# Moving one modulation vector's load and sums from a feed-forward to the token mixer of the second layer

## The chip, the cores and the metric

The kernel runs on one core of one Trainium2 chip. The metric is the device time of one execution in microseconds (us), as the median of several runs. Five engines work side by side, each through its own instructions in order: TensorE (PE, matmuls, with weight loads shown apart as PEld), VectorE (DVE), ScalarE (ACT), GpSimd (POOL) and SyncE (SP), which here only issues DMA transfers from HBM.

## What is computed

Two layers of a decoder trunk on 256 rows of width 1024, in f32. In each layer three sub-layers follow each other: a SwiGLU feed-forward, a token mixer with two attention branches, and a second feed-forward. Each is wrapped in a modulated norm and a gated residual:

```python
c_act = jax.nn.silu(c)
for l in range(DEPTH):
    mod = c_act @ w_ada[l] + b_ada[l]                 # 9 vectors of 1024
    sh1, sc1, g1, sh2, sc2, g2, sh3, sc3, g3 = jnp.split(mod, N_MOD, axis=-1)
    x = x + 0.5 * g1[:, None, :] * swiglu(modulate(x, sh1, sc1), ffn1_gate[l], ffn1_up[l], ffn1_down[l])
    x = x + g2[:, None, :] * token_mix(modulate(x, sh2, sc2), ...)
    x = x + 0.5 * g3[:, None, :] * swiglu(modulate(x, sh3, sc3), ffn2_gate[l], ffn2_up[l], ffn2_down[l])
return rms_norm(x) * final_norm
```

`modulate(x, shift, scale)` is `rms_norm(x) * (1 + scale) + shift`. The nine vectors of `mod` are numbered 0 to 8 in the code. The change is about number 6 of the second layer, `sh3`, which is first needed by the norm ahead of that layer's second feed-forward.

## The kernel before

**Products.** Every f32 matrix is used as a high and a low part. A weight is loaded into a buffer named `raw` (128 x 2048 values at most, usually 1 MB, 4 buffers in a ring), and `split_unit` makes the two parts of it: ScalarE copies the high one (`whi`, line 177), VectorE subtracts for the low one (`wlo`, line 179). PE then does three products per pair of tiles (line 105). A `raw` buffer is free for the next load when its splits are done.

**Modulation vectors.** `ada_half` makes half a vector (512 values). It loads two blocks of 1 MB of `w_ada` (line 216) into the same ring of `raw` buffers, and VectorE adds 4 columns of each to an accumulator `acc`, so 8 sums per half (line 222 for the first, which only multiplies and is shorter, line 224 for the others). `finish` then adds over the partitions: for the gate vectors (2, 5, 8) by two products with ones, for the others by a column sum, 8 tiny matmuls on PE `tr<-acc,ones`, and three small VectorE instructions (`mcol`, `cs`, `col`). A vector so takes 4 loads, 16 sums and, if it isn't a gate, 2 column sums.

**Where they run.** Each sub-layer is given a list of halves (`HALVES`), and `ada_load` makes a generator of it. The sub-layer's code calls `ada_step` at fixed places, mostly just after it has issued the load of a weight, and each call runs the generator to its next `yield`. In a feed-forward the steps stand in the gate and up products (13 of them in the second layer's first feed-forward) and then one behind the load of each block of the down weight (`stream_units`, line 435, `ada_every` = 1); one step issues a load and then its sums. What is left runs before the norm (`ada_flush`). The feed-forward named has 10 halves before the change, so 20 loads, of which the last 7 are issued in the down projection. In the token mixer the flag `ada_lag` is set: `ada_half` yields between the load and its sums, and once more behind the sums. Its first four steps stand behind the loads of the 408-column products (two: gates and latent query, buffers `cqs`) and of the 288-column products (two: latent key and value, `cks`); the next ones stand at lines 718, 752 and 802, two in the query products, and so on. Before the change the first layer's token mixer has 2 halves there (vector 7), and the second layer's none.

**The order on the engines.** Instructions of each engine are put in order by a scheduler ahead of time, from the program's order and its own estimate of durations; on the chip each engine keeps that order and waits on semaphores. SP's queue of loads is in order too: a load that waits for a free `raw` buffer holds up those behind it.

Of the kernel before, what the change touches and what calls it, by code (L numbers as in the profile page):

```python
# [77 lines left out]
def hybrid_trunk(ctx, tc, t, out):  # L78
# [20 lines left out]
    def trps():  # L99
        return psum.tile([P, 512], F32, name="tr", tag="tr", bufs=2)  # L100
# [3 lines left out]
    def mm(o, a, b, start, stop):  # L104
        last_mm[0] = nc.tensor.matmul(o, a, b, start=start, stop=stop)  # L105
# [29 lines left out]
    def raw_tile():  # L135
        return raws.tile([P, 2048], F32, name="raw", tag="raw")
# [49 lines left out]
    def column_sums(ps, vec, a, start, stop):  # L186

        av = a.rearrange("p (j i r) -> p j i r", j=4, i=4)
        for i in range(4):
            mm(ps[32 * i:32 * i + 32, :P].rearrange("p (j r) -> p j r", j=4), vec, av[:, :, i, :], start, stop)  # L190

    def pick_columns(ps):
        m = small.tile([P, 4, 32], F32, name="mcol", tag="mcol", bufs=1)
        nc.vector.tensor_tensor(m, ps[:, :P].rearrange("p (j r) -> p j r", j=4),
                                colmask[:, None, :].to_broadcast([P, 4, 32]), ALU.mult)
        cs = small.tile([P, 4], F32, name="cs", tag="cs", bufs=2)
        nc.vector.tensor_reduce(cs, m, AX.X, ALU.add)
        return cs

    def add_bias(l, ch, n, cs):  # L200
        if (l, ch) not in mods:
            mods[l, ch] = small.tile([P, KD], F32, name="col", tag="col", bufs=8)
        nc.vector.scalar_tensor_tensor(mods[l, ch][:, n * 4:n * 4 + 4], cs, 1.0 if ch in (1, 4, 7) else 0.0,
                                       bcols[:, l, ch * 8 + n * 4:ch * 8 + n * 4 + 4], ALU.add, ALU.add)

    def ada_half(l, ch, n):
        acc = keep.tile([P, 512], F32, name="acc", tag="acc", bufs=2)
        row = ch in (2, 5, 8)
        n0 = ch * D + n * 512
        wv = t["w_ada"][l].rearrange("(p j) n -> p j n", p=P)  # L210
        if row:
            nc.scalar.dma_start(binit[0:1, :], t["b_ada"][l:l + 1, n0:n0 + 512])
        for j in range(0, KD, 4):
            r = raw_tile()
            rv = r.rearrange("p (j n) -> p j n", j=4)
            nc.sync.dma_start(rv, wv[:, j:j + 4, n0:n0 + 512])
            if ada_lag[0]:
                yield
            for jj in range(4):
                cj = cact[:, j + jj:j + jj + 1]  # L220
                if j + jj == 0 and not row:
                    nc.vector.tensor_scalar_mul(acc, rv[:, jj, :], cj)
                else:
                    nc.vector.scalar_tensor_tensor(acc, rv[:, jj, :], cj, binit if j + jj == 0 else acc,  # L224
                                                   ALU.mult, ALU.add)
            yield
        if row:
            if n == 0:
                mods[l, ch] = keep.tile([P, D], F32, name="g", tag="g", bufs=2)
            hi, lo = (scr.tile([P, 512], F32R, name="acc%d" % i, tag="uf", bufs=2) for i in range(2))  # L230
            nc.scalar.activation(hi, acc, AF.Copy)
            nc.vector.tensor_tensor(lo, acc, hi.bitcast(F32), ALU.subtract)

            def finish():
                ps = trps()
                mm(ps, ones, hi, True, False)
                mm(ps, ones, lo, False, True)
                nc.scalar.activation(mods[l, ch][:, n * 512:(n + 1) * 512], ps, AF.Copy, scale=1.0 if ch == 5 else 0.5)
        else:
            def finish():  # L240
                ps = trps()
                column_sums(ps, ones[:, :32].bitcast(F32), acc, True, True)
                cs = pick_columns(ps)
                add_bias(l, ch, n, cs)
        ada_late.append(finish)

    ada_late = []
    ada_lag = [False]
    ada_gen = [None]

    def ada_load(chunks):
        def g():
            for l, ch, n in chunks:
                for _ in ada_half(l, ch, n):
                    yield
                    while ada_late:
                        ada_late.pop(0)()
            while ada_late:
                ada_late.pop(0)()
        ada_gen[0] = g()  # L260
# [858 lines left out]
    HALVES = lambda l, *chs: [(l, ch, n) for ch in chs for n in range(2)]  # L1119
# [15 lines left out]
    def start_norm(l, sub):  # L1135
        u = new_u()

        def post(hf):
            pending.append([DELAY[hf] + (sub == 1 and hf == 1), norm_mod(hf, u[0], u[1], mods[l, 3 * sub + 1], mods[l, 3 * sub],
                                                sub == 1 and hf == 1)])  # L1140
        return u, post
# [41 lines left out]
    for i, (l, sub) in enumerate(subs):  # L1183
        u = nxt
        if i + 1 < len(subs):
            state = {}

            def post(hf, state=state, ls=subs[i + 1]):
                if hf == 0:
                    state["u"], state["post"] = start_norm(*ls)  # L1190
                state["post"](hf)
        else:
            post = final_norm
        if sub == 0:
            ffn(l, 1, u[0], u[1], HALVES(l, 2, 3, 4, 5, 6), post,
                xn if l == 0 else None, small_columns if l == 0 else None)
        elif sub == 1:
            token_mix(l, u[0], u[1], HALVES(l, 7) if l == 0 else [], post)
        else:
            ffn(l, 2, u[0], u[1], HALVES(l, 8) + (HALVES(l + 1, 1, 0, 7) if l + 1 < DEPTH else []), post)  # L1200
        if i + 1 < len(subs):
            nxt = state["u"]
# [22 lines left out]
```

## Time and profile before

| what | value |
|---|---|
| median of 3 runs | 1177.66 us (1175.4 to 1183.46) |
| the profiled execution | 1180.38 us, its span from first to last instruction 1178.6 us |
| busy: PE, PEld, DVE, ACT | 97%, 86%, 80%, 54% of the span |
| bytes moved | 274.95 MB, 233 GB/s on average |
| mean granted TensorE clock | 0.995 of full speed |

The stages can be told by what PE multiplies. In the second layer the first feed-forward's down projection begins near 731 us and ends near 791, the token mixer's first products begin near 796, its 408-column products at 821, its 288-column products at 830, and the second feed-forward's down projection runs from 1111 to the end. The first layer's token mixer has its 408-column products at 247 and its 288-column products at 256, and the second feed-forward of that layer its down projection from 540 to 598. The times in the rows below are us from the start of the span. A recorded matmul is longer than the time to the next one's start, since they are pipelined; what a matmul costs in a row of them is the difference of two starts.

### The profile page before, as it was taken

To read this page: it belongs to the slowest core of one execution; us is meant where nothing else is said; L and a number is where in the kernel's file an instruction comes from. 1 tells how busy PE (TensorE), PEld (TensorE's weight loads), DVE (VectorE), ACT (ScalarE), POOL (GpSimd) and SP (SyncE) were. 2 spreads that over 40 slices of the span, in tenths; PEclk is the share of its full clock that TensorE was granted. 3 is DMA by queue.
4 is the path that set the end of the run, shared out by engine and by line. 5 is a ranking of instruction groups with operands and counts; after the bars stand their busy time and mean duration, and the time that the engine had idled before them with its cause. 6 is when DMAs were issued, how large, how long until landed. Compare 5 with 4: busy or idle time off the path is not lost.

```text
span 1178.6 us, 20227 instructions
## 1 busy us (share of the span) xinstructions
PE 1145.7 (97%) x7902; PEld 1007.8 (86%) x7902; DVE 938.5 (80%) x1889; ACT 641.2 (54%) x1156; POOL 2.6 (0%) x16
## 2 busy tenths in 40 slices
PE   4999999999999999999999999999999999999997
PEld 3799987789977889998879999877997778999985
DVE  4888899779897898799578879975888888865553
ACT  4444436647677564444455534356677756564441
POOL 0000000000000000000000000000000000000000
PEclk9999999999999999999999999999999999999999
DMA  9989999686823578989838979976574354986530
GB/s 327 325 295 306 318 357 330 218 223 182 249 73 108 181 230 303 315 272 323 293 119 286 314 250 347 336 253 170 148 215 108 108 170 152 305 252 212 184 138 36
DMA packets 201970, 274.95 MB, mean 233 GB/s; under 512 B 13613, under 2 KB 119815, under 8 KB 201875
## 3 DMA queue, kind: packets, MB, share of 16 engines
q1 hardware_dynamic: 201119, 273.02, 70.8%
q8 instruction: 62, 1.02, 0.3%
q10 hardware_dynamic: 756, 0.64, 0.2%
q14 instruction: 33, 0.27, 0.1%
HBM read 272.60 MB, written 1.05 MB: 232 GB/s over the span
## 4 chain that ended last, share of the span: by engine, by line
PE 60%; DVE 18%; DMA 14%; ACT 4%; issue 3%; SPq 1%; DVEq 0%; ACTq 0%
PE mm L105 52%; DVE wlo L179 8%; DVE acc L224 4%; DMA raw<-in_ffn_up 4%; DMA raw<-in_w_ada 4%; DMA raw<-in_ffn_down 3%; PE tr L108 3%; ACT whi L177 2%; PE sc L105 2%; PE po L105 2%; DMA raw<-in_ffn_gate 2%; PE tr L105 1%; DVE hf L497 1%; DVE hl L499 0%; DVE rtmp L455 0%
## 5 line engine op out<-in xcount | busy, mean ns | idle before, releaser
L179 DVE TENSOR_TENSOR wlo<-raw,whi 128x1024 fp32r<-128x1024 f32 (+5 forms) x400 | 423.4, 1074 | 125.0 <-ACT whi L177 122.2
L177 ACT ACTIVATE whi<-raw 128x1024 fp32r<-128x1024 f32 (+5 forms) x400 | 364.4, 936 | 231.2 <-PE mm L105 90.4
L105 PE MATMUL mm<-uhi,whi 128*128 128x256 f32 x1248 | 346.6, 278 | 0.0
L105 PE MATMUL mm<-uhi,wlo 128*128 128x256 f32 x1248 | 345.2, 277 | 0.7 <-DVE wlo L179 0.7
L105 PE MATMUL mm<-ulo,whi 128*128 128x256 f32 x1248 | 344.9, 276 | 0.0
L105 PEld LDWEIGHTS mm<-uhi,whi 128*128 128x128 f32 x1248 | 234.3, 188 | 2.7 <-issue 1.4
L105 PEld LDWEIGHTS mm<-uhi,wlo 128*128 128x128 f32 x1248 | 234.3, 188 | 1.1 <-DVE wlo L179 1.0
L105 PEld LDWEIGHTS mm<-ulo,whi 128*128 128x128 f32 x1248 | 234.5, 188 | 0.5
L224 DVE SCALAR_TENSOR_TENSOR acc<-raw,cact,acc 128x512 f32<-128x512 f32 x224 | 167.3, 748 | 6.6 <-DMA raw<-in_w_ada 3.7
L105 PE MATMUL mm<-wlo,hh 128*128 128x512 f32 x352 | 137.6, 391 | 2.1 <-DVE wlo L179 2.1
L105 PE MATMUL mm<-whi,hh 128*128 128x512 f32 x352 | 138.3, 393 | 0.0
L105 PE MATMUL mm<-whi,hl 128*128 128x512 f32 x352 | 137.1, 389 | 0.0
L105 PE MATMUL mm<-whi,uhi 128*128 128x512 f32 (+3 forms) x336 | 127.2, 380 | 3.4 <-ACT uhi L557 2.6
L105 PE MATMUL mm<-whi,ulo 128*128 128x512 f32 (+3 forms) x336 | 126.5, 377 | 1.3 <-DVE ulo L345 1.3
L105 PE MATMUL mm<-wlo,uhi 128*128 128x512 f32 (+3 forms) x336 | 125.7, 374 | 0.0
L498 ACT ACTIVATE hh<-hf 128x256 fp32r<-128x256 f32 x70 | 29.2, 417 | 103.7 <-DVE hf L497 103.7
L105 PEld LDWEIGHTS mm<-wlo,hh 128*128 128x128 f32 x352 | 66.1, 188 | 16.9 <-DVE wlo L179 3.6
L105 PEld LDWEIGHTS mm<-whi,hh 128*128 128x128 f32 x352 | 66.1, 188 | 15.2 <-ACT whi L177 0.9
L105 PEld LDWEIGHTS mm<-whi,hl 128*128 128x128 f32 x352 | 66.1, 188 | 13.6
L105 PEld LDWEIGHTS mm<-whi,uhi 128*128 128x128 f32 x336 | 63.7, 190 | 14.7 <-ACT uhi L557 3.0
L105 PEld LDWEIGHTS mm<-whi,ulo 128*128 128x128 f32 x336 | 64.0, 190 | 12.2 <-DVE ulo L345 3.2
L105 PEld LDWEIGHTS mm<-wlo,uhi 128*128 128x128 f32 x336 | 64.0, 190 | 9.3 <-issue 0.3
(248 smaller groups left out, 1328.9 us busy)
## 6 DMA issues: line engine op xcount, KB each, us to landing
raw<-in_w_ada SPq DMA_DIRECT2D x72, 1024.0 KB, 9.2
raw<-in_ffn_gate SPq DMA_DIRECT2D x41, 1024.0 KB, 6.1
raw<-in_ffn_up SPq DMA_DIRECT2D x41, 1024.0 KB, 6.0
raw<-in_ffn_down SPq DMA_DIRECT2D x40, 1024.0 KB, 8.2
raw<-in_w_in SPq DMA_DIRECT2D x18, 1024.0 KB, 5.5
raw<-in_w_in SPq DMA_DIRECT2D x16, 512.0 KB, 5.2
raw<-in_w_out SPq DMA_DIRECT2D x8, 1024.0 KB, 5.6
raw<-in_ffn_down SPq DMA_DIRECT2D x8, 512.0 KB
```

The lines of the kernel that those rows point to most:

```text
L105: last_mm[0] = nc.tensor.matmul(o, a, b, start=start, stop=stop)
L108: nc.tensor.transpose(o, a, ident)
L177: nc.scalar.activation(a, s, AF.Copy)
L179: nc.vector.tensor_tensor(b, s, a.bitcast(F32), ALU.subtract)
L224: nc.vector.scalar_tensor_tensor(acc, rv[:, jj, :], cj, binit if j + jj == 0 else acc, ALU.mult, ALU.add)
L497: nc.vector.tensor_tensor(hf32, ps[:, 256:], sg, ALU.mult)
L498: nc.scalar.activation(h[0][:, f, :], hf32, AF.Copy)
```

## The change

Vector 6 of the second layer leaves the list of that layer's first feed-forward (8 halves stay, 16 loads) and becomes the list of its token mixer, which had none. And in the token mixers the second of the two `yield`s goes: a step now does the sums of the load before and at once issues the next load, and one more `yield` at the end of the list takes the last column sum a step further on. So the four loads of a vector are issued in the first four steps there, where they took steps 1, 3, 5 and 7. This holds for the first layer's vector 7 and for the second layer's vector 6. In the feed-forwards the flag is off, and their steps are as before.

```diff
@@ ada_half
                     nc.vector.scalar_tensor_tensor(acc, rv[:, jj, :], cj, binit if j + jj == 0 else acc,
                                                    ALU.mult, ALU.add)
-            yield
+            if not ada_lag[0]:
+                yield
@@ ada_load
                     yield
                     while ada_late:
                         ada_late.pop(0)()
+            if ada_lag[0]:
+                yield
             while ada_late:
                 ada_late.pop(0)()
@@ the list of sub-layers
         if sub == 0:
-            ffn(l, 1, u[0], u[1], HALVES(l, 2, 3, 4, 5, 6), post,
+            ffn(l, 1, u[0], u[1], HALVES(l, *((2, 3, 4, 5, 6) if l == 0 else (2, 3, 4, 5))), post,
                 xn if l == 0 else None, small_columns if l == 0 else None)
         elif sub == 1:
-            token_mix(l, u[0], u[1], HALVES(l, 7) if l == 0 else [], post)
+            token_mix(l, u[0], u[1], HALVES(l, 7 if l == 0 else 6), post)
```

On SP, in the second layer's token mixer, the loads stood so before the change (the loads of the 408- and 288-column weights, small ones of the compression, and those of the next products):

```order
L435 DMA raw<-in_w_in 128x4x408
L776 DMA w_9340<-in_cmpk_w 64x64
L776 DMA w_9340<-in_cmpv_w 64x64
L435 DMA raw<-in_w_in 128x4x408
L435 DMA raw<-in_w_in 128x4x288 x2
L717 DMA raw<-in_w_in 128x8x256
L750 DMA raw<-in_w_in 128x8x128
L751 DMA raw<-in_w_in 128x8x128
```

and stand so in the changed kernel (lines behind the edits are 3 higher):

```order
L438 DMA raw<-in_w_in 128x4x408
L779 DMA w_9340<-in_cmpk_w 64x64
L779 DMA w_9340<-in_cmpv_w 64x64
L216 DMA raw<-in_w_ada 128x4x512
L438 DMA raw<-in_w_in 128x4x408
L216 DMA raw<-in_w_ada 128x4x512
L438 DMA raw<-in_w_in 128x4x288
L216 DMA raw<-in_w_ada 128x4x512
L438 DMA raw<-in_w_in 128x4x288
L216 DMA raw<-in_w_ada 128x4x512
L720 DMA raw<-in_w_in 128x8x256
```

One modulation load now stands behind each of the four weights. In the first layer's token mixer the same four places hold one each after the change, where before they held one behind the first and one behind the third weight, and two further on.

On VectorE, at the same place of the second layer, the low parts of the 408-column weights (128x816) and of the 288-column weights (128x576) and the copies out of PSUM (`gate`, `cqs`) stood in this order before:

```order
L179 TENSOR_TENSOR wlo<-raw,whi 128x816 x4
L179 TENSOR_TENSOR wlo<-raw,whi 128x576 x3
L694 TENSOR_SCALAR gate<-gate 128x24
L695 COPY cqs<-mm 128x384
L694 TENSOR_SCALAR gate<-gate 128x24
L695 COPY cqs<-mm 128x384
```

and in the changed kernel in this one, from the second 128x816 split on:

```order
L224 SCALAR_TENSOR_TENSOR acc<-raw,cact,acc 128x512
L179 TENSOR_TENSOR wlo<-raw,whi 128x816
L224 SCALAR_TENSOR_TENSOR acc<-raw,cact,acc 128x512
L179 TENSOR_TENSOR wlo<-raw,whi 128x816
L224 SCALAR_TENSOR_TENSOR acc<-raw,cact,acc 128x512 x2
L222 TENSOR_SCALAR acc<-raw,cact 128x512
L224 SCALAR_TENSOR_TENSOR acc<-raw,cact,acc 128x512 x3
L179 TENSOR_TENSOR wlo<-raw,whi 128x576
L224 SCALAR_TENSOR_TENSOR acc<-raw,cact,acc 128x512 x2
L179 TENSOR_TENSOR wlo<-raw,whi 128x576
L224 SCALAR_TENSOR_TENSOR acc<-raw,cact,acc 128x512 x2
```

The sums of the second load stand between the 408-column splits, all four of the third ahead of the first 288-column split, and those of the fourth around the second one; a third 288-column split and the copies follow. The first layer's token mixer has the same order there.

## Rows read from the trace of the kernel before

**Rows 1.** Busy time of the engines, from the page: us, share, instructions.

```profile
PE 1145.7 (97%) x7902; PEld 1007.8 (86%) x7902; DVE 938.5 (80%) x1889; ACT 641.2 (54%) x1156; POOL 2.6 (0%) x16
```

**Rows 2.** Table by windows: stretch, length, busy us (instructions) by engine, clock, DMA share, GB/s.

```profile
731.00:796.00 65.00, 64.18 (x301) 51.39 (x296) 55.43 (x84) 31.65 (x46) 0.00 (x0) 1.00 0.86 297
540.00:603.00 63.00, 62.42 (x297) 50.52 (x296) 42.49 (x63) 30.70 (x43) 0.00 (x0) 1.00 0.67 235
247.30:263.50 16.20, 15.48 (x97) 15.22 (x96) 9.46 (x17) 7.86 (x15) 0.00 (x0) 1.00 0.83 219
821.30:836.60 15.30, 15.30 (x98) 15.26 (x97) 7.23 (x12) 7.80 (x15) 0.00 (x0) 1.00 0.72 168
1110.70:1170.00 59.30, 59.30 (x264) 49.11 (x263) 26.46 (x33) 21.39 (x28) 0.00 (x0) 1.00 0.31 107
```

**Rows 3.** PE by time, second layer's first feed-forward: start, us, what, [idle before <-releaser].

```profile
768.35 0.39 PE L105 MATMUL mm<-whi,hl 128*128 128x512 f32 x1
...
769.10 0.50 PE L105 MATMUL mm<-whi,hh 128*128 128x512 f32 x1
770.36 0.50 PE L105 MATMUL mm<-wlo,hh 128*128 128x512 f32 x1 [0.76 <-DVE wlo L179]
```

**Rows 4.** Chain that ended last, in order of time, same place: start, us, what.

```profile
758.01 9.89 DMA raw<-in_ffn_down
...
769.08 1.24 DVE wlo L179
```

**Rows 5.** Line 224, all sums but the first of a half: ns min/median/max, first and last start.

```profile
L224 DVE SCALAR_TENSOR_TENSOR acc<-raw,cact,acc x224: 740/747/754, 63.5 to 1031.5; 128x512 f32<-128x512 f32 x112
```

**Rows 6.** PE by time at a column sum of the first layer's token mixer.

```profile
268.94 0.28 PE L105 MATMUL mm<-ulo,whi 128*128 128x256 f32 x1
269.06 0.28 PE L105 MATMUL mm<-uhi,wlo 128*128 128x256 f32 x1
...
269.63 0.38 PE L105 MATMUL mm<-uhi,whi 128*128 128x256 f32 x1
```

**Rows 7.** DVE by time, the first 288-column split of the second layer.

```profile
824.47 0.76 DVE L179 TENSOR_TENSOR wlo<-raw,whi 128x576 fp32r<-128x576 f32 x1 [6.03 <-ACT whi L177]
```

**Rows 8.** DVE by time, the same split of the first layer and the sum behind it.

```profile
250.43 0.76 DVE L179 TENSOR_TENSOR wlo<-raw,whi 128x576 fp32r<-128x576 f32 x1 [3.00 <-ACT whi L177]
253.90 0.49 DVE L222 TENSOR_SCALAR acc<-raw,cact 128x512 f32<-128x512 f32 x1 [2.72 <-DMA raw<-in_w_ada]
```

**Rows 9.** Chain that ended last, in order of time, first layer's 288-column products.

```profile
246.67 0.76 DVE acc L224
...
247.45 6.43 DMA raw<-in_w_ada
...
257.76 0.59 ACT junk L697 x2
```

**Rows 10.** PE by time, the same products.

```profile
257.38 0.29 PE L105 MATMUL mm<-whi,uhi 128*128 128x288 f32 x1
258.39 0.40 PE L105 MATMUL mm<-whi,uhi 128*128 128x288 f32 x1 [0.72 <-ACT junk L697]
```

**Rows 11.** SP by time, first layer's token mixer: from the first issue's start to the last's end.

```profile
230.14 5.32 SPq L435 DMA_DIRECT2D raw<-in_w_in  x2
238.57 0.37 SPq L216 DMA_DIRECT2D raw<-in_w_ada  x1
```

**Rows 12.** PE by time, down projection of the first layer's second feed-forward.

```profile
557.13 0.39 PE L105 MATMUL mm<-whi,hl 128*128 128x512 f32 x1
558.10 0.43 PE L105 MATMUL tr<-acc,ones 128*32 128x128 f32 x8 [0.58 <-DVE acc L224]
```

## The prediction

> **What bounds the kernel now.** I read the totals first: TensorE (PE) shows 97% busy, VectorE (DVE) 80%, ScalarE 54% [rows 1]. Such a PE row hides short waits, because a matmul's recorded span overlaps the next one's. So I went to stretches: the table by windows, and in it the number of matmuls per time [rows 2]. The last window (down projection of the last feed-forward, where no modulation load runs) is the measure: 264 products of 512 columns in 59.30 us, 0.225 us each, and nothing waits. The same projection in the second layer's first feed-forward, the stretch that the change lightens, takes a 65 us window for 301 instructions; in the first layer's second feed-forward, which already has the load plan that the change gives to the other (16 loads instead of 20), a 63 us window for 297. I laid both windows from the first product of the projection to the fifth or so of the next stage, rounded to a microsecond, so their difference of 2.0 us is good to about half a microsecond. PE is therefore the bound nearly everywhere, and what the change can move are its few small gaps. I looked for these in PE's instructions by time, and read what ended them in the chain of waits.
>
> In the stretch that gets lighter there are two kinds. A column sum (eight tiny matmuls that turn an accumulator into columns) costs PE its own time and the start of the next weights: 768.35 to 769.10 is 0.75 us for one product and one group, so 0.53 for the group [rows 3]. Right behind it PE stands once more: 769.10 to 770.36 is 1.26 us, 1.03 over the pace [rows 3]. The chain says why: the split of a down weight waited for its 1 MB load, issued at 758.01 and 9.89 us under way, directly behind the issue of the last modulation load on the same queue [rows 4].
>
> **The change, part by part.**
>
> *Removed from the second layer's first feed-forward:* loads 17 to 20 of its plan, all in the down projection; 16 sums on DVE, 16 x 0.747 = 12.0 us [rows 5], and two column sums on PE. DVE is busy 55.43 of 65 us there [rows 2], so its 12 us are not PE's. What PE gets back are the two groups (0.53 for the one shown; the other I put at 0.45, the price of a group in [rows 6], below) and, as the forecast has it, the 1.03 us of the late down weight, since four loads fewer stand in its queue: -2.0. Bounds: -0.9 if only the groups go; -2.9 if every gap of the stretch goes. The latter comes from PE's weight loads: they took 49.11 of 59.30 us where nothing waited (82.8%), so the 51.39 us of this stretch need 51.39 / 0.828 = 62.1 of its 65.0 us [rows 2]. The 2.0 between the two like stretches agrees with the middle.
>
> *Added to the second layer's token mixer:* the same four loads and sums at the four steps of the 408- and 288-column products. DVE has the room: before the first 288-column split it now sits idle 6.03 us [rows 7], and in this whole stretch it works 7.23 of 15.30 us [rows 2]. DMA engines were 0.72 busy there. So bytes and DVE time are hidden. PE pays two groups: in the first layer 269.06 to 269.63 is 0.57 us, less the 0.12 that a product of 256 columns takes there, 0.45 [rows 6]: +0.9.
>
> *The wait that comes with it.* DVE runs in order, and in the new order the first two sums of the fourth load stand ahead of the second 288-column split and the other two ahead of the third; behind them all stand the copies that empty the PSUM bank of the 408-column products, for which PE waits. The first layer shows this today with its third load. The load was issued at 247.45, the moment the last sum of the load before gave its buffer back, landed 6.43 us later, and DVE had been idle 2.72 us before the sum at 253.90 [rows 8, 9]. The splits, the copy and ScalarE's square followed late, and PE stood from 257.38 to 258.39: 1.01 us less the 0.13 of a product, 0.88 [rows 9, 10]. In the second layer, which has no such loads, the same 288-column split ran at 824.47 against 250.43, a fixed distance of 574.04 us [rows 7, 8], and 15.30 us sufficed for what took 16.20 [rows 2].
>
> After the change both layers have the denser form. In the first layer's times: the second load moves up from 238.57 to the place of the first 288-column weight, 230.14 + 5.32 - 0.37 = 235.09 [rows 11]. Of its four sums two now stand ahead of the last 408-column split, so the last of them ends about 2 x 0.75 = 1.5 us before the present 247.4, and the load that then takes its buffer (the fourth) is issued near 245.9 and, at the same 6.43 us, lands near 252.4, 1.5 us earlier than the third does now. Behind it DVE has four full sums instead of one short and two full ones, about 1.0 us more. Net 0.5 earlier than today: a PE gap of about 0.4 to 0.5 instead of 0.88. First layer: -0.4 (bounds -0.9, the gap gone, and the same excess as in the first rival). Second layer: +0.5 (bounds 0, as its own trace of today, and the first rival's price). The first layer's two column sums only change place, and its third and fourth load leave a stretch further on in which I find no PE gap that they caused: 0, both ways by no more than one such gap, 0.5.
>
> *The lag itself* changes nothing elsewhere: the flag is set only inside the token mixer, and there the sums already ran one step behind their load. What is new is that the next load is issued in the step of the sums, so that four loads take five steps instead of eight.
>
> **Sum:** -2.0 + 0.9 + 0.5 - 0.4 = -1.0 us. The profiled execution took 1180.38 us (span 1178.6), 2.7 above the median of the runs, 1177.66. 1180.38 - 1.0 = 1179.4 for an execution like it; on the median's footing 1176.7.
>
> **Rivals.** *The fourth load comes late (slower).* Price: if these loads need the 9.89 us of [rows 4] instead of 6.43, the fourth lands 3.5 us later by itself, and nearly as much again because the second load, too, is late for its first sum, so that its buffer comes free about 3.5 us later. A gap of 0.5 becomes 7 or so in each layer: (7 - 0.9) + 7 + 0.9 - 2.0 = +12 us, 1190 on the median's footing. With only the landing late, 4 us each: +6, 1184. It speaks for this that bytes per step grow: 816 or 576 KB of weights and 1024 KB of modulation in each step. Against it: in the first layer today a 1 MB weight is issued 3 us ahead of the late load, and in the new order a 576 KB one, so that the queue ahead is no longer. It turns the sign when the fourth load is about half a microsecond slower than 6.43. Chance 0.20, of which 0.03 for more than 1%.
>
> *The down weight is late anyway.* If the 9.89 us are the down weights' own time, the 1.03 stays: -1.0 + 0.9 + 0.5 - 0.4 = 0, 1177.7. For it: the first layer's second feed-forward has a gap as well, 557.13 to 558.10 with an idle of 0.58 [rows 12]. Against it: that one waits for a sum and not for a weight. Chance 0.13.
>
> *PE has far more room than the gaps show.* A stage's PE headroom could be what its weight loads leave free: 65.0 - 51.39 = 13.6 us, and if taking DVE work and bytes away freed it, the time would be 1164. The row against it: the window with no wait at all has weight loads 82.8% of the time and is at PE's pace [rows 2]. Chance 0.02. The Trainium skill (Perfetto Trace Analysis, Identifying the Most-Contended Engine) has this as a rule: judge PE's headroom by the busy share of weight loads, not of matmuls. By it the sum would be -13.6 at best; the trace agrees that the matmul share misleads, but not that 100% is the mark for these products.
>
> *No gap at all in the token mixers* (both go to 0): -2.0 + 0.9 - 0.9 = -2.0, 1175.7. Chance 0.08.
>
> **How the numbers follow.** The forecast, between -2.0 and 0, has 0.57; the others 0.20, 0.13, 0.02 and 0.08. The likeliest time is 1176.7. The range 1173.0 to 1182.0 goes down past the best case by what the runs of before scatter around their median (2.3 us downwards) and up to a gap of 3 to 4 us in each layer, and leaves out the worst landing, the headroom rival and an unlucky median. About 1%, 11.8 us, is what a measurement of this kernel can tell from no change; only the headroom rival, and the late load at its worst, reach that. Faster 0.02, within 1% 0.95, slower 0.03.
>
> **What would show each step.** In the changed kernel: no column sum between the products near 762 and 769, and no wait of a down weight there (else the second rival); a window of about 63 us for that down projection; two new groups of 0.45 in the second layer's token mixer; the fourth load about 10.8 us behind the second in both token mixers and about 6.4 us under way (9 or more: the first rival); a PE gap ended by ScalarE's square of 0.3 to 0.7 us in both layers. A PE gap of several microseconds in the 288-column products, or one further on because the buffer ring runs late for the next weights, would make the prediction wrong.

## The result

The changed kernel took 1189.3 us (median of 9 runs, 1180.08 to 1191.8), the kernel before beside it 1177.89 (9 runs, 1175.4 to 1183.46). The ratio is 1.0081, interval [1.0061, 1.0101]: slower, by about 10 us, where 1176.7 was forecast, and above the range. Timed once more, in 12 runs, it took 1184.97 beside 1177.66: 1.0063 [1.0042, 1.0084].

The profiled execution has a span of 1188.0 us, 9.4 over that of before. The totals hardly show it. From the page (busy us, share, instructions), to hold against [rows 1]:

```profile
PE 1148.2 (97%) x7902; PEld 1010.7 (85%) x7902; DVE 938.1 (79%) x1889; ACT 641.6 (54%) x1156; POOL 2.5 (0%) x16
```

The table by windows does show it. These are the stretches of [rows 2] and two short ones that come up below (columns as there: stretch, length, then PE, PEld, DVE, ACT, POOL, granted clock, DMA share, GB/s):

```profile
734.80:802.10 67.30, 64.14 (x281) 52.16 (x277) 43.34 (x61) 31.52 (x46) 0.00 (x0) 0.97 0.65 222
244.40:265.50 21.10, 17.66 (x106) 16.93 (x105) 12.43 (x22) 7.87 (x15) 0.00 (x0) 0.92 0.91 229
827.50:845.80 18.30, 16.14 (x106) 15.48 (x106) 12.21 (x22) 7.78 (x15) 0.00 (x0) 1.00 0.95 242
257.70:261.00 3.30, 3.25 (x15) 3.26 (x16) 2.13 (x4) 2.28 (x5) 0.00 (x0) 0.60 1.26 264
756.50:760.00 3.50, 3.50 (x11) 2.67 (x10) 1.33 (x2) 0.38 (x1) 0.00 (x0) 0.53 1.05 387
```

The first row is the down projection of the second layer's first feed-forward. It lost 12 us of VectorE work (55.43 to 43.34) and 20 matmul records (301 to 281; the two column sums are 16 of them), and yet takes 67.3 us instead of 65. The next two are the 408- and 288-column products of the two token mixers: 21.1 us (16.2 before) and 18.3 (15.3). Elsewhere the two executions agree but for scatter of about 1 us a stage, and 2.3 us in one that the change does not touch, the first layer's first down projection. Three stages thus hold the loss: +4.81 and +2.97 us in the 288-column products, from the first of them to the first product of the next stage, and +2.62 in the down projection.

**First and second place: the 288-column products.** TensorE by time in the first layer (start, us, what, [idle before <-releaser]), which answers [rows 10]:

```profile
254.01 0.29 PE L105 MATMUL mm<-whi,ulo 128*128 128x288 f32 x1
257.75 0.40 PE L105 MATMUL mm<-whi,uhi 128*128 128x288 f32 x1 [3.44 <-ACT junk L700]
```

Between 254.01 and 257.75 no product starts: 3.60 us over the pace, 0.88 before. (Gaps below are always start to start, less the pace.) The chain that ended last, in order of time, says why; it answers [rows 9]:

```profile
243.03 9.08 DMA raw<-in_w_ada
...
252.20 0.76 DVE acc L224
...
256.62 0.47 DVE cqs L698
...
257.11 0.59 ACT junk L700 x2
```

The fourth load is 9.08 us under way, not 6.43. Its sums stand on VectorE ahead of the copy `cqs` (L698) that empties the bank, and TensorE waits for that bank. In the second layer the same happens; VectorE by time there:

```profile
834.04 1.54 DVE L224 SCALAR_TENSOR_TENSOR acc<-raw,cact,acc 128x512 f32<-128x512 f32 x2 [2.58 <-DMA raw<-in_w_ada]
```

From its issue at 826.16 that is 7.88 us to the first sum, and the TensorE gap is 2.32 us. The issues of the first layer, SP by time, answer [rows 11]:

```profile
232.25 0.37 SPq L216 DMA_DIRECT2D raw<-in_w_ada  x1
...
241.59 0.37 SPq L438 DMA_DIRECT2D raw<-in_w_in  x1
243.03 0.37 SPq L216 DMA_DIRECT2D raw<-in_w_ada  x1
246.34 0.37 SPq L720 DMA_DIRECT2D raw<-in_w_in  x1
```

The second load (232.25) and the fourth (243.03) are 10.78 us apart, as worked out ahead. New are the neighbours: a 576 KB weight 1.44 us ahead of the fourth load, and a 1 MB weight 3.31 us behind it, whose buffer the third load's sums had just given back.

**Third place: a wait nobody looked for.** TensorE in the second layer's first feed-forward, around the last two column products of its shortened list (the gate vector's second half, `ones` with its high and with its low part):

```profile
751.52 0.39 PE L105 MATMUL mm<-whi,hl 128*128 128x512 f32 x1
752.29 0.50 PE L105 MATMUL tr<-acc,ones 128*128 128x512 f32 x1 [0.39 <-ACT acc L232]
755.57 0.50 PE L105 MATMUL tr<-acc,ones 128*128 128x512 f32 x1 [2.77 <-DVE acc L233]
```

VectorE by time, the same place:

```profile
747.70 1.54 DVE L224 SCALAR_TENSOR_TENSOR acc<-raw,cact,acc 128x512 f32<-128x512 f32 x2
749.15 5.76 DVE L179 TENSOR_TENSOR wlo<-raw,whi 128x1024 fp32r<-128x1024 f32 x5
754.83 0.68 DVE L233 TENSOR_TENSOR acc<-acc,acc 128x512 fp32r<-128x512 f32 x1
```

The sums end at 749.2. The subtraction that makes the low part stands behind five weight splits, 5.76 us, and ends at 755.5. With no step left in the list, both products were traced right behind it, and TensorE meets them at 751.74: 0.55 + 3.04 us of waiting. In the kernel before the list went on with vector 6, so this half was finished a step later; the low part stood behind two splits there, and TensorE hardly waited (VectorE, then TensorE by time; the next product starts at 754.34, 0.34 us over the pace of two):

```profile
753.26 0.69 DVE L232 TENSOR_TENSOR acc<-acc,acc 128x512 fp32r<-128x512 f32 x1
753.55 0.95 PE L105 MATMUL tr<-acc,ones 128*128 128x512 f32 x2
```

**And behind two of the three gaps the clock.** The two short rows of the table above have granted clocks of 0.60 and 0.53; behind these gaps TensorE ran for some 3 us at a granted clock of 0.5, the 1.2 GHz level. Products of 512 columns start 0.43 us apart there instead of 0.227. Nothing of the kind stands behind the 2.32 us gap.

### The profile page after: what moved, and what is told of

The parts are those of the page before. It is cut to its first block, busy times and chain, and to the rows that moved or that the text cites. A ratio compares the mean times of both kernels' runs of the same rounds, so it can differ in the third digit from the quotient of the medians.

```text
span 1188.0 us, 20232 instructions
## 1 busy us (share of the span) xinstructions
PE 1148.2 (97%) x7902; PEld 1010.7 (85%) x7902; DVE 938.1 (79%) x1889; ACT 641.6 (54%) x1156; POOL 2.5 (0%) x16
## 4 chain that ended last, share of the span: by engine, by line
PE 74%; DVE 11%; DMA 8%; ACT 3%; issue 3%; SPq 1%; DVEq 0%; ACTq 0%
PE mm L105 66%; DVE wlo L179 4%; DMA raw<-in_w_ada 4%; PE tr L108 3%; DMA raw<-in_ffn_up 3%; DVE acc L224 2%; PE sc L105 2%; PE po L105 2%; ACT whi L177 2%; PE tr L105 1%; DMA raw<-in_ffn_down 1%; DMA raw<-in_ffn_gate 1%; ACT junk L299 0%; DMA c_in<-in_c 0%; DVE hf L500 0%
## 5 line engine op out<-in xcount | busy, mean ns | idle before, releaser
L224 DVE SCALAR_TENSOR_TENSOR acc<-raw,cact,acc 128x512 f32<-128x512 f32 x224 | 167.0, 747 | 10.8 <-DMA raw<-in_w_ada 7.8
```

## The experiments

My theory had three parts, each against a rival: the token mixers lose by VectorE's order behind a late load (and not by the load as such), the feed-forward loses by the early finish, and the load is late because of the load behind it. Each time is the median of 12 runs, but "next load held" of 9 and "fourth load alone" of 2, and the kernel before was run 28 to 35 times beside them. The first four kernels ran on one chip, the other eight on another.

| kernel | us | before beside it | ratio, interval |
|---|---|---|---|
| lag alone | 1178.93 | 1177.42 | 1.0008 [0.9990, 1.0025] |
| move alone | 1181.91 | 1177.42 | 1.0043 [1.0025, 1.0060] |
| changed, sums behind | 1179.87 | 1177.42 | 1.0024 [1.0005, 1.0043] |
| changed, finish late | 1180.33 | 1177.42 | 1.0017 [1.0001, 1.0034] |
| changed, again | 1184.97 | 1177.66 | 1.0063 [1.0042, 1.0084] |
| changed, next load held | 1183.39 | 1177.66 | 1.0052 [1.0029, 1.0075] |
| both waits away | 1176.46 | 1177.66 | 0.9986 [0.9972, 1.0001] |
| the same, every list late | 1174.85 | 1177.66 | 0.9987 [0.9973, 1.0001] |
| changed, fourth load alone | 1186.07 | 1176.58 | 1.0078 [1.0048, 1.0109] |
| move, every list late | 1176.25 | 1176.58 | 0.9996 [0.9977, 1.0015] |
| every list late, no change | 1177.01 | 1176.58 | 0.9998 [0.9983, 1.0013] |
| both waits away, no move | 1175.55 | 1176.58 | 0.9994 [0.9980, 1.0009] |

**The lag alone** (the two hunks with `yield`, lists as before).

> The kernel before with the two yield edits alone; both lists stay as before, so the second layer's token mixer has no loads and its first feed-forward keeps all twenty. Theory (in the token mixer VectorE stands in line behind the fourth load's sums, and the PSUM bank that the 288-column products want is copied out by VectorE behind them): the first layer's 288-column stretch takes about 12.1 us as in the changed kernel, against 7.3 before, with one TensorE gap of about 3.5 us ahead of its last products and a granted clock of 0.5 behind it; the second layer as before; in all +4 to +5 us over the kernel before. Rival (what was lost comes from the moved vector and the second layer): within 1 us of the kernel before, 288-column stretch under 8 us. Rival (the stretches of two executions differ by themselves): stretch neither 12 nor 7.

Measured: +0.9 us, less than I had said, and its interval holds no change. The gap is there in the first layer, but smaller:

```profile
255.53 0.29 PE L105 MATMUL mm<-whi,ulo 128*128 128x288 f32 x1
257.73 0.40 PE L105 MATMUL mm<-whi,uhi 128*128 128x288 f32 x1 [1.90 <-ACT junk L700]
```

2.06 us over the pace, no fall of the clock, a stretch of 9.07 us. The fourth load took 7.63 us to its first sum, not 9.17. So the place is right and the size differs from one execution to the next: neither 12 nor 7, and the rival of scatter holds part of the truth.

**The move alone** (the two list hunks).

> The kernel before with the two list edits alone: vector 6 moved, the sums right behind their loads as before. Theory (in the second layer's first feed-forward the last half of the shortened list is finished right behind its sums, its low part stands behind five weight splits on VectorE, and TensorE waits for it): the two column sums near 752 us again with about 0.4 and 2.8 us of waiting ahead of them, and a granted clock of 0.5 behind, so that the down projection takes 67.3 us against 64.7; the first layer's token mixer as before (288-column stretch about 7.3 us), the second layer's with a gap of about 0.9 us; in all +3 to +5 us over the kernel before. Rival (all of it is the lag): -1 to -2 us, no such wait.

Measured: +5.1 us by the ratio (the "+4.3 us" in two expectations further on is the 0.43% misread as microseconds), with the wait where it was expected, and nothing of note in the token mixers (stretches of 6.88 and 6.62 us):

```profile
746.32 0.49 PE L105 MATMUL tr<-acc,ones 128*128 128x512 f32 x1 [0.59 <-ACT acc L231]
747.93 0.50 PE L105 MATMUL tr<-acc,ones 128*128 128x512 f32 x1 [1.12 <-DVE acc L232]
```

0.75 + 1.39 us over the pace, then a stretch at a clock of 0.5; the down projection takes 65.82 us.

**The changed kernel with the sums behind the copies.**

```diff
-    nc.vector.tensor_copy(cqs[:, hf, :], ps[:, 24:408])
+    last_cq[0] = nc.vector.tensor_copy(cqs[:, hf, :], ps[:, 24:408])
...
+    behind = ada_lag[0] and n == 1 and j == 4
+    with tc.issue_after(last_cq[0].ins) if behind else contextlib.nullcontext():
         (the sums of this load)
```

> The changed kernel with the sums of the fourth load queued on VectorE behind the two copies that empty the banks of the 408-column products. Theory (it is VectorE's order and not the transfer that holds TensorE): the fourth load still lands late (7.8 to 9 us), yet no TensorE gap over 1 us ahead of the last 288-column products in either layer, no granted clock of 0.5 there; that stretch falls from 12.1 to about 7 and from 9.3 to about 6.8 us; in all 6 to 7.5 us under the changed kernel. Rival (the late landing only moves the wait: the buffer comes free later, so the load behind it is issued later, and its products wait): less than 4 us gained, a new gap of 2 us or more in the products behind.

Measured: no gap in either 288-column stretch. The table by windows, first and second layer:

```profile
254.20:261.10 6.90, 6.90 (x57) 6.54 (x57) 6.14 (x14) 4.89 (x9) 0.00 (x0) 1.00 0.95 226
828.10:835.00 6.90, 6.90 (x57) 6.54 (x57) 6.14 (x14) 4.89 (x9) 0.00 (x0) 1.00 0.93 221
```

TensorE is busy in all of 6.90 us. The load's last packets still start 6.9 to 7.0 us behind its issue, so it is no earlier. What follows takes 0.6 us more in one stage and 0.7 less in the next: the wait was not moved. Against the changed kernel the gain is 0.0039, 4.6 us, by its second timing (1.0063), and 6.7 us by its first (1.0081); the intervals are too wide to say whether the 6 to 7.5 us forecast were right. The windows carry the theory: with the load as late as before and its sums behind the copies the gaps are gone, so VectorE's order holds TensorE.

**The changed kernel with the finish one step later** in the second layer's first feed-forward.

```diff
-            if ada_lag[0]:
+            if ada_lag[0] or chunks[-1][:2] == (1, 5):
                 yield
             while ada_late:
```

> The changed kernel with the last half of the second layer's first feed-forward finished one step later: 24 products stand ahead of its two column sums. Theory (TensorE waits there for the low part, 0.5 + 3.0 us, and then works for 3.4 us at half the clock, 1.6 us): no wait over 0.3 us at these sums, no granted clock of 0.5 near 756, the down projection 4.5 to 5 us shorter (67.3 to about 62.6); in all -4.5 to -5 us against the changed kernel, the token mixers as in it. Rival (another wait, for a down weight or a PSUM bank, takes its place): less than 3 us gained.

Measured: the wait is gone. The down projection as a window, and one behind a gap of this execution:

```profile
729.00:790.90 61.90, 61.90 (x281) 51.08 (x278) 43.30 (x61) 31.86 (x46) 0.00 (x0) 1.00 0.71 244
829.30:832.70 3.40, 3.40 (x17) 3.40 (x15) 2.12 (x3) 1.74 (x4) 0.00 (x0) 0.50 1.30 247
```

61.9 us, TensorE busy throughout; 0.0046 under the changed kernel's second timing, 5.4 us (7.5 by the first). The second row is the second layer's token mixer, whose 288-column gap was 2.76 us this time, with half the clock behind it: its stretch took 11.29 us.

**The changed kernel again.** The expectation speaks of the chip of the first four kernels; it ran on the other.

> The changed kernel, timed beside the three below and on the chip of the first four experiments. The parts alone gave +0.9 us (lag) and +4.3 us (move), together +5.2; the changed kernel with either wait taken away came to +2.8 (sums behind the copies) and +2.0 (finish one step later). Theory A (the two waits add up, and what they cost differs from one execution to the next): about 1182 to 1184 us in the median here, with single times from 1178 to 1190. Rival B (the two waits feed each other, each costs more in the presence of the other): 1187 to 1190 again, +9 to +11.

Measured: 1184.97, +7.4 us by the ratio, between the two and nearer to theory A. Its windows (down projection, then the two 288-column stretches):

```profile
732.80:799.80 67.00, 64.20 (x281) 52.23 (x278) 42.69 (x60) 31.34 (x46) 0.00 (x0) 0.97 0.64 222
254.50:265.30 10.80, 8.72 (x59) 7.83 (x58) 7.36 (x15) 4.96 (x10) 0.00 (x0) 0.84 1.14 234
834.10:842.90 8.80, 7.19 (x58) 6.59 (x58) 6.75 (x14) 4.94 (x10) 0.00 (x0) 1.00 1.18 240
```

Each stage is over its undisturbed length (61.9, 6.9, 6.9) by 5.1, 3.9 and 1.9 us, 10.9 together. The two cures took off 5.4 and 4.6, together 10.0. The parts alone came to 0.9 + 5.1 = 6.0; what neither of them holds is the lag in the second layer's mixer, 1.9 here. So the stages add up to about what the cures took off, and nothing in them shows the waits feeding each other. The medians alone leave it open: the two cures together ("both waits away" below) took off 9.1 us by the second timing of the changed kernel and 11.2 by the first, where the sums of the single cures are 10.0 and 14.2.

**The next load held.** The 1 MB weight behind the fourth load starts when that has landed:

```diff
...
+            nc.gpsimd.tensor_copy(r[:, :1], last_load[0][:, :1])
...
             nc.sync.dma_start(rv, w_in[:, :, 512:768])
```

> The changed kernel in which the 1 MB load behind the fourth one (of w_in columns 512 to 768, issued some 3 us behind it) starts only when the fourth has landed: GpSimd copies one column of the fourth load's buffer into the next load's buffer first. Theory (the fourth load is late because that next load shares the DMA engines with it): the fourth load's first sum starts 6.4 us or less behind its issue in both layers (7.2 to 9.2 in the five sightings so far), VectorE's idle time ahead of it falls from 1.9 to 3.9 us to about 1, the TensorE gap in the 288-column stretch to 1 us or less, no granted clock of 0.5 there; 2 to 4 us under the changed kernel in the same call. Rival (what lies ahead of it in the queue makes it late): still 7.2 us or more, same gaps, and the held load comes late as well.

Measured: the theory falls for the most part. SP and then VectorE, second layer:

```profile
819.91 0.37 SPq L216 DMA_DIRECT2D raw<-in_w_ada  x1
828.24 0.37 SPq L722 DMA_DIRECT2D raw<-in_w_in  x1
```

```profile
827.42 1.54 DVE L224 SCALAR_TENSOR_TENSOR acc<-raw,cact,acc 128x512 f32<-128x512 f32 x2 [2.21 <-DMA raw<-in_w_ada]
```

With nothing behind it the fourth load still needed 7.51 us (6.93 in the first layer), against 7.24 to 9.17, mean 7.91, of the seven sightings with the load behind (a sighting is one layer of one profiled execution). By these means the load behind costs about 0.7 us, but the 7.51 lies within the range of the seven. The DMA packets of the traces, which also cover the kernels whose sums are queued behind, say less: the last 2 KB packet of the fourth load ended 6.62 to 7.85 us behind its issue in fourteen sightings with the load behind (mean 7.09), and 6.54 and 6.96 in the two without. Gaps of 1.39 and 1.95 us stay.

**The fourth load alone**: as above, and it also waits until the 576 KB weight ahead of it has landed.

> The version in which the load behind the fourth is held, with the fourth load itself held too: it starts when the 576 KB load ahead of it (the second of the 288-column weights, issued 1.4 us ahead of it) has landed, by the same one-column copy on GpSimd. Held behind alone gave 6.9 and 7.5 us from its issue to its first sum, against 7.2 to 9.2 (mean 7.9 of seven) with a load behind it and 6.4 in the kernel before. Theory (it shares the DMA engines with the load just ahead of it): issued some 2.7 us later, it needs 5.5 us or less from its issue, like the 1 MB load of the kernel before that has 5.5 between issue and landing; so it lands no earlier, and the TensorE gap stays at 2 to 3 us. Rival (a load of this shape takes 7 us whatever is beside it): 7 us or more from its issue, a gap of 4 us or more.

Measured, SP and VectorE in the second layer:

```profile
822.07 0.37 SPq L219 DMA_DIRECT2D raw<-in_w_ada  x1
```

```profile
827.88 2.33 DVE L227 SCALAR_TENSOR_TENSOR acc<-raw,cact,acc 128x512 f32<-128x512 f32 x3 [1.45 <-DMA raw<-in_w_ada]
```

5.81 us here, 5.16 in the first layer. So the larger part of its lateness is the load 1.44 us ahead of it: 5.2 to 5.8 us alone, 6.9 to 7.5 behind that load, 7.2 to 9.2 with both neighbours. The 9.17 stands apart: in the other eight sightings behind a neighbour the first sum started 0.4 to 0.6 us behind the load's last 2 KB packet, but here the last packet ended at 7.03 us and the landing came at 9.08. What held it is open.

That the distance counts, and not the bytes, can be read from the executions with the order of the kernel before, in which a 1 MB weight is issued 3.0 us ahead of the third modulation load and nothing close behind it: there the last packet ended 4.67 to 5.98 us behind the issue in six sightings (5.98 is the row from which the 6.43 was taken), 4.64 and 5.40 alone, and 6.54 and 6.96 with the 576 KB weight 1.44 us ahead. The gaps of the version with the load alone came out smaller than said (0.77 and 1.41 us), as the scheduler now put three sums and not four ahead of the first copy; what it saved there was lost further on, at the held 1 MB weight (2.8 to 3.4 us more in the next stage).

**Both waits away**, the two cures together, and **the same with every list finished late** (the condition of the late `yield` dropped).

> The changed kernel with both waits taken away: the fourth load's sums behind the two bank copies, and the last half of the second layer's first feed-forward finished one step later. Theory: the down projection of the second layer 61.9 to 62.5 us (64.7 before), its 288-column stretch about 6.9 (6.35 before), the first layer's about 6.9 (7.34 before), no TensorE gap over 1 us in these stages; the rest of the second token mixer +0.5 to +1 over before; in all 1.0 to 2.5 us under the kernel before. Rival (something else in the change costs several us): as slow as the kernel before or slower.

> As the version with both waits taken away, but every list's last half is finished one step later, so those of the first layer's feed-forwards and of the last one too. Theory (the short wait of 0.58 us for a low part at the end of the first layer's second feed-forward is of the same kind): that wait gone too, 0.3 to 1.5 us under the version with both. Rival (in the first layer no step is left behind the last half, so it is finished at the very end of the products, where TensorE has nothing else to do): 0.5 to 2 us over it.

Measured: 1176.46 and 1174.85 beside 1177.66. The first is as expected in size; the second is 1.6 us under it by the medians and level with it by the ratios (0.9987 and 0.9986), so its saving is not shown, though the wait it was meant for is gone (the first layer's second down projection took 62.25 us, and 63.57 in the first of the two). The intervals of both hold 1. Windows of the second (down projection, 288-column stretches):

```profile
726.60:788.60 62.00, 62.00 (x281) 51.15 (x278) 43.30 (x61) 31.79 (x46) 0.00 (x0) 1.00 0.69 241
253.20:260.10 6.90, 6.90 (x58) 6.54 (x57) 6.15 (x13) 4.89 (x9) 0.00 (x0) 1.00 0.98 233
822.90:829.80 6.90, 6.90 (x57) 6.54 (x57) 6.14 (x14) 4.89 (x9) 0.00 (x0) 1.00 0.95 226
```

**Is it the moved vector that pays?** Three kernels: the move with every list late; every list late and nothing else; both waits away without the move.

> The kernel before with the two list edits, and every list's last half finished one step later (the move alone gave +4.3 us, with waits of 0.75 + 1.39 us and half the clock behind them in the second layer's first feed-forward). Theory (that wait is all that the move costs beyond what it gives): -1 to +1 us against the kernel before; no wait at those column sums, down projection of the second layer about 62 us, its 288-column stretch 6.6, the rest of its token mixer +0.5 to +0.9. Rival (the move costs something else): +2 us or more.

> The kernel before with nothing of the change: only, every list's last half is finished one step later. Theory (the second layer's first feed-forward has no step left behind its last half in the long list; only the short wait of 0.58 us in the first layer's second feed-forward is there to be saved): 0 to -1 us against the kernel before. Rival (finishing late is what made the best version fast): -2 to -3 us.

> The best version so far (both waits away, every list finished one step later: 1174.85 us beside 1177.66) with the lists of the kernel before, so that no vector is moved. Theory (the moved vector gives back in the second token mixer what it saves in the feed-forward: -1.2 of column sums against +0.9): within 1 us of the best version, 1 to 3 us under the kernel before. Rival (the moved vector is what makes the best version faster): level with the kernel before, within 0.5 us.

Measured: 0.9996, 0.9998 and 0.9994, all level with the kernel before. The third cannot tell its theory from its rival: 0.7 us by the ratio, with an interval from 2.4 us under to 1.1 over. The move costs nothing once its wait is gone, and gives nothing that can be measured. In the stages it does what was said: the down projection takes 61.91 us with the short list and 63.15 with the long one, 1.24 less. But the long list has a second length, which the third kernel's trace does not show and the second's does:

```profile
766.07 0.49 PE L105 MATMUL mm<-whi,hh 128*128 128x512 f32 x1 [0.53 <-ACT whi L177]
767.32 0.50 PE L105 MATMUL mm<-wlo,hh 128*128 128x512 f32 x1 [0.76 <-DVE wlo L179]
```

The late down weight of [rows 3, 4] came in two of four executions with the long list (64.66 and 65.09 us), and not in the others (63.15 twice).

## Why the prediction was wrong

- **The feed-forward, -2.0.** The removal did what the sum said: the two column sums are gone, and no weight came late there. Measured without the new wait it is -2.75 against the profile of before, -1.24 against an execution without the late weight, so the term was fair. What failed is that the list's new last half got no price. The changed kernel took +2.62 us there (+2.26 in the second profile): 3.59 us of waiting and about 1.6 of clock.
- **The pattern had been in a row.** [Rows 12] shows a column sum waiting for its last sum at the end of a list, 0.58 us. The prediction read it only as evidence on the down weight ("waits for a sum and not for a weight") and did not ask which half would become the last one in the shortened list. With every list finished a step later, that projection took 62.25 to 62.26 us in all four traces; in the ten others it took 62.24 to 63.92.
- **The token mixers, +0.5 and -0.4.** The order was foreseen: which sums stand ahead of which split, the bank, ScalarE's square, and the issue 10.8 us behind the second load. The failed step is "at the same 6.43 us". Nine sightings (seven of the changed issue order, two with the next load held) put the gap at the landing less 5.56 us, within 0.02: 9.17 gave 3.60, 7.24 gave 1.68, 6.93 gave 1.39. (Here the landing is the first sum's start, counted from the issue.) At 6.43 it would have been 0.87, so even that figure left nothing of the -0.4. The reason is a second thing that the sum left out: TensorE meets the bank that is still to be emptied after six 288-column products, where it met it after ten before, 0.53 us sooner. The first of them in the first layer, before and after; the last ones ahead of the gap start at 257.38 [rows 10] and 254.01:

```profile
256.19 0.30 PE L105 MATMUL mm<-whi,uhi 128*128 128x288 f32 x1
253.35 0.30 PE L105 MATMUL mm<-whi,uhi 128*128 128x288 f32 x1
```

- **The rival that came true** is the first one, with a chance of 0.20: the place and the late landing were right. Its second part, a second load that is late too, did not come (10.77 to 10.80 us between the two issues in every trace with the changed order, but for the kernel that holds the fourth load back), and with 0.87 at 6.43 the sum had no half microsecond to spare before it turned. What spoke against it, "the queue ahead is no longer", counted bytes ahead. What counted is how close the neighbours are in time: the load 1.44 us ahead (most of it), and perhaps the load behind, which the sum did not look at. The Trainium skill (DMA: Bandwidth & Descriptors, Queues, rings and completion order) says that each DMA engine takes descriptors in ring order and that a load's semaphore lands only after that engine's earlier writes; 5.2 to 5.8 us alone against 6.9 to 7.5 behind a neighbour agrees with it, though no run here looked at single engines.
- **The two column sums, +0.9.** 0.45 each stands: the second mixer's stages without a gap are together about 0.9 us longer (+0.55, +0.08, 0.00 and +0.22 in the version with both waits away).
- **The clock.** No term held it: 1.6 us a time, in up to two places of an execution.
- **More room for TensorE** (1164) fell: TensorE had nothing to give. By the rule of the Trainium skill (Perfetto Trace Analysis, Identifying the Most-Contended Engine) weight loads of 51.08 in 61.90 us would still leave 17%; the row has TensorE busy in all of it, at its pace, as [rows 2] had shown.
- **The range** reached to 1182 with gaps of 3 to 4 us in both mixers. Gaps of about that size came (3.60 and 2.32) and alone would have stayed inside it (1177.7 - 2.0 + 0.9 + 2.7 + 2.3 = 1181.6); the unseen wait and the clock took the time out.

## To carry to other kernels

When work is taken off the end of a list, ask what becomes its last entry and whether anything still lies between its sums and the engine that consumes them; one empty step at the end of the list was worth about 5 us here. Ahead of a copy that empties a PSUM bank, put nothing on an in-order engine that waits for a transfer: queue it behind, and the transfer may land when it likes. And take the time of a load from a row with the same neighbours, ahead and behind, not from a row with the same size.

## What the runs showed of the hardware

TensorE's granted clock fell to half behind some short gaps and not behind others of like length. In the 288-column products, with TensorE at full pace ahead of each gap, it fell behind gaps of 3.60, 2.76, 2.24 and 1.95 us, and not behind 2.32, 2.06, 1.77, 1.68, 1.41 and 1.39. In the feed-forward it fell behind 0.55 + 3.04, 2.22 + 1.01, 1.73 + 1.01 and 0.75 + 1.39 us (two gaps with one product between; in the third pair already inside the second gap), and not behind 2.35 + 1.01, nor behind a single one of 2.19. Before it, TensorE stood idle; while it lasted, TensorE was fully busy again. The price is steady: a 288-column stretch took 6.90 us, plus its gap, plus 0.1 where the clock stayed, and plus 1.56 to 1.65 where it fell (12.15, 11.29, 10.70 and 10.43 us). That a waiting TensorE is slowed and activity restores it is what the Trainium skill says (TensorE: Matmul & The Clock Gate, What's actually happening); that it follows a gap of 2 us in one execution and not in the next is probably part of why the changed kernel scatters: 1177 to 1193 us in twelve runs, against 1175 to 1179 in the twelve of the version with both waits away.
